# Time mixing in a two-layer decoder trunk: TensorE's rows in program order, weight products cut into units, weights stored in pieces

## The chip, the cores and the metric

The kernel runs on one core of one Trainium2 chip. The metric is device time in microseconds of one execution, the median of several runs. A core has five engines that each work through a queue in order: TensorE (PE, with its weight loads as PEld), VectorE (DVE), ScalarE (ACT), GpSimd (POOL) and SyncE (SP, which here issues the weight DMAs).

## The reference

The trunk has two layers over 256 tokens of width 1024. Layer 0 is RWKV-7 time mixing with memory attention, then a dense SwiGLU; layer 1 is a chunked gMLP with memory attention, then eight experts. What matters here is layer 0's mixing:

```
p = rms_norm(x) @ w_in               # 2816 columns: r, k, v (768 each), lora 256, q 256
r, k, v, wd, ad, gd = split(token_shift_lerp(p))
step:  s = s * w_t - (s @ kk_t) (kk_t * a_t) + v_t k_t ;  y_t = s @ r_t   # 12 heads, 256 steps
y = (group_norm(y) * lnx_w + lnx_b + bonus(r, k) * v) * g
k_m, v_m = split(rms_norm(mem) @ w_kv_mem[i])             # for both layers i
o = softmax(q @ k_m.T / 8) @ v_m                          # 4 heads, 256 memory tokens
x = x + concat(y, o) @ w_out
```

## The kernel before, in words

Every activation is held transposed, 128 features by 256 tokens. A weight product is done in one of two ways. Split: ACT writes a weight piece's rounded part `hi` (L127), DVE the rest `lo` (L128), and TensorE makes three products (hi with high activations, lo with high, hi with low; `lin_cm`, `lin_tm`). Whole: TensorE multiplies the raw float32 weights directly, each product of which the trace shows as two rows. Split pieces go through four buffers of 128x512 per side, so a piece of the next block waits until TensorE has done with the piece four before it. `project(c0, whole)` loads 256 columns of `w_in` (one megabyte) and gives a function that makes its 2 x 128 output rows; `WHOLE` says which blocks are whole: lora, the first two k blocks, all three v blocks. A raw weight lands in one of two or three buffers by a DMA that SP issues in written order.

The recurrence is done in chunks of 64 tokens, 4 chunks of 12 heads (24 pairs of heads, `NM`). After the k blocks, `ND` holds in-chunk products (`AR`, `BK`; 32x32 tiles); DVE transposes them to `NL` (L597) and solves a triangular system in 15 steps of a product and a reduce each (`prod` L605, `TT` L607), transposes the answer twice (`T` L610, `T32t` L611), and TensorE completes it in three passes of 96 small products, `within` (first `T,W`, then `Z,T32t` and `T32t,Z`, the last two each followed by an addition on DVE). The r blocks give `rT`, `AR` and `bt` on DVE and the bonus sums `mm<-bt,bones`; `G` is 48 products of `AR` and `BK` masked on DVE; the v blocks give `vT`, then `VU`; four rounds build `Q` and `VU`; a loop carries the state `S`; `ys` and `group_norm` give y. Only then are the memory tokens normed and turned (`m_tm`), and `mem_kv` and `mem_attn` run.

All engines but SP are ordered by the framework's scheduler, from the program order and tile dependences; SP keeps the written order. TensorE's rows of this stage are therefore not in program order: r blocks stand among the k blocks' work, and the first v block stands while DVE solves the system.

Of the kernel before, what the change touches and what calls it, by code (L numbers as in the profile page):

```python
# [17 lines left out]
D = 1024  # L18
T = 256
# [11 lines left out]

@with_exitstack
def trunk(ctx: ExitStack, tc: tile.TileContext, a: dict, out: bass.AP, dbg=None, full=True):
    nc = tc.nc
    pe, dve, act, pool, sp = nc.tensor, nc.vector, nc.scalar, nc.gpsimd, nc.sync
    dbg = dbg or (lambda name, ap: None)

# [49 lines left out]
    class Stream:  # L87
# [24 lines left out]
        def fetch_cols(self, w, c0, n):  # L112

            if self.early:
                return self.early.pop(0)
            kk = min(KD, 2048 // n)
            return [self.fetch(w[k * 128:(k + kk) * 128, c0:c0 + n].rearrange("(k p) f -> p k f", p=128))
                    for k in range(0, KD, kk)]
# [32 lines left out]
        def rows(self, w, k0, nk):  # L151

            for k in range(k0, k0 + nk, 2):
                n = min(2, k0 + nk - k)
                v = self.fetch(w[k * 128:(k + n) * 128, :].rearrange("(k p) f -> p k f", p=128))
# [194 lines left out]
    def mem_kv(ws_, i, mh):  # L350

        for p in banks_cm(ws_, a["w_kv_mem"][i], 0, 256, mh, 256):
            act.activation(flat(KT[i]), p, AF.Copy)
        yield
        w = ws.cols(a["w_kv_mem"][i], 256, 256)
# [86 lines left out]
    w_in = a["rwkv_w_in"][0]  # L442
# [14 lines left out]
    def project(c0, whole):  # L457

        if c0 == MIX + 256:
            ws.raws.append(rawb)  # L460
        elif c0 == 2 * MIX:
            ws.raws = [raw0, rawb]
        if not whole:
            if not n1:
                split_n1()
            us = list(ws.blocks(w_in, c0, 256))
        else:
            v = ws.fetch_cols(w_in, c0, 256)[0]

        def products():  # L470
            p = lin_bank()
            for j in range(2):
                o = p[:, j * T:j * T + T]
                if not whole:
                    lin_cm(o, us[j], n1)
                for k in range(KD if whole else 0):
                    mm(o, v[:, k, j * 128:j * 128 + 128], n1f[:, k, :], k == 0, k == KD - 1)
            return p
        return products

    WHOLE = {'l': (1,), 'k': (1, 1, 0), 'v': (1, 1, 1), 'r': (0, 0, 0), 'q': (0,)}
    rawb = lambda: rl.tile([128, 2048], F32, name="rawb", tag="rawb")
    projs = (f() for f in ahead(project(c0 + 256 * i, w) for c0, n in ((2304, "l"), (MIX, "k"), (0, "r"), (2 * MIX, "v"), (2560, "q"))
             for i, w in enumerate(WHOLE[n])))
    lora = rb.tile([128, 2, T], F32, name="lora")
    p = next(projs)
# [46 lines left out]
    for i in range(3):  # L533
        p = next(projs)
# [28 lines left out]
    kstack.close()  # L563

# [47 lines left out]

    def within(left, right):
# [15 lines left out]
    rm = rms(m_tm, bv.rearrange("p b t -> p (b t)")[:, None, :D].to_broadcast([128, 2, D]), False)  # L629
    for i in range(3):  # L630
        p = next(projs)
        pb = mm_bank()
        for j in range(2):
            b = 2 * i + j
            rT = f256("rT")
            lerp(rT, p[:, j * T:(j + 1) * T], b)
            dve.tensor_tensor(AR[:, b, :, 1, :], rT.rearrange("p (c j) -> p c j", c=NC), c4(PD, b), op=ALU.mult)
            t = f256("bt")
            dve.scalar_tensor_tensor(t.rearrange("p (c j) -> p c j", c=NC), AR[:, b, :, 1, :], P("rwkv_r_k", b),
                                     BK[b][:, :, 1, :], op0=ALU.mult, op1=ALU.mult)  # L640
            mm(pb[:, j * T:j * T + T], bones, t, True, True)
        act.activation(bv[:, 2 * i:2 * i + 2, :], pair(pb), AF.Copy)

    G = ra.tile([128, 2, NM, 128], F32, name="G", tag="pack")
    for b in range(NB):
        ps = [acc_bank().rearrange("p (c i) -> p c i", c=NC) for _ in range(2)]
        for c in range(NC):
            for s in range(2):
                h = halves[s]
                mm(ps[s][:, c, :], flat(BK[b][h, c, s:s + 2, :]), flat(AR[h, b, c, :, :]), True, True)  # L650
        for s in range(2):
            dve.tensor_tensor(G[:, s, b * NC:(b + 1) * NC, :], ps[s],
                              gmask[:, None, :].to_broadcast([128, NC, 128]), op=ALU.mult)


    vT = rb.tile([128, NB, T + CH], F32, name="vT")
    for i in range(3):
        p = next(projs)
        for j in range(2):
            lerp(vT[:, 2 * i + j, :T], p[:, j * T:(j + 1) * T], 12 + 2 * i + j)  # L660
    qT = rb.tile([128, 2, T], F32, name="qT")
    act.activation(flat(qT), next(projs), AF.Copy)
    for b in range(0, NB, 2):
        act.activation(vT[:, b:b + 2, T:], vT[:, b:b + 2, 0:CH], AF.Copy)
# [9 lines left out]

    for c in range(1, NC):
        p = mm_bank().rearrange("p (b v) -> p b v", v=CH)
        for b in range(NB):
            for h in halves:
                mm(p[h, b, :], AR[h, b, c, 0, :], ident[h, h], True, True)
        act.activation(AR[:, :, c, 0, :], p[:, :NB, :], AF.Copy)  # L680
    VU = ra.tile([128, 2, NM, CH], F32, name="VU", tag="kr")
    slot = lambda s, c: (c + 1) % NC if s else c
    for b in range(NB):
        p = mm_bank().rearrange("p (w d) -> p w d", w=4)
        for w in range(4):
            f = (w + 3) % 4
            mm(p[:, w, :], vT[:, b, f * CH:f * CH + 128], cent, True, True)
        act.activation(VU[0:64, 1, b * NC:(b + 1) * NC, :], p[0:64, :, 64:128], AF.Copy)
        act.activation(VU[64:128, 0, b * NC:(b + 1) * NC, :], p[64:128, :, 0:64], AF.Copy)
# [10 lines left out]
    for p, (m0, m1) in zip(pz, runs):  # L700
        act.activation(Z2[32:64, m0:m1], p[32:64, :m1 - m0], AF.Copy)
        dve.tensor_copy(Z2[96:128, m0:m1], p[96:128, :m1 - m0])
    pz = banks2()
# [7 lines left out]
    dbg("TT", TT.rearrange("p a b -> p (a b)"))  # L711
    sstack.close()
# [17 lines left out]
    for c in range(NC):  # L730
        if c:
# [19 lines left out]
    for c in range(NC):  # L751
        if c + 1 < NC:
            p = state(acc_bank)
            for b, s, h in heads:
                mm(p[h, b, :], BKt[:, s, b * NC + c, :], VU[:, s, b * NC + slot(s, c), :], b == 0, c == 0 and b == NB - 1, True)
            for b, s, h in heads if c else ():
                mm(p[h, b, :], AR[h, b, c, 0, :], S[c - 1][h, b, :], False, b == NB - 1, True)
            dve.tensor_tensor(S[c], p[:, :NB, :], PC[:, :, c, None].to_broadcast([128, NB, CH]), op=ALU.mult)
        if c:
            p = state(acc_bank)  # L760
# [604 lines left out]
```

## Time and profile before

| | |
|---|---|
| median of 3 runs | 1333.71 us (1330.75 to 1334.09) |
| profiled execution | 1332.82 us, its span 1330.7 us, mean granted TensorE clock 0.985 |
| TensorE busy | 1291.1 us (97%) |
| VectorE / ScalarE busy | 1027.7 us (77%) / 898.1 us (67%) |
| layer 0, time mixing and memory attention | from 44 to 218 us of the span, products with `w_out` behind it |
| dense SwiGLU | about 245 to 435 us |
| gMLP layer and routing | about 435 to 525 us |
| experts | about 525 to 1316 us |

A window row gives the busy time of each engine in a stretch, with the number of its instructions, the granted clock and the DMA engines' mean share. TensorE's products are pipelined and their ends are modelled, so its pace is read from starts or counts.

### The profile page before, as it was taken

Reading aid. Unit: us, or ns where it says so; the run is one execution under the profiler, and the core shown is the slowest. Engines: PE = TensorE matmul, PEld = TensorE weight load, DVE = VectorE, ACT = ScalarE, POOL = GpSimd, SP = SyncE. Lnnn points to the kernel's source line nnn. Section 1 sums busy time; section 2 is a strip of 40 time slices with the busy share of each in tenths; the row PEclk is TensorE's granted clock in tenths of the full one; section 3 lists DMA queues with packets and bytes.
Section 4 is the critical chain, followed back from the end, with each engine's and each line's share of the span. In section 5 each row is a group of like instructions: output and inputs, shape, how many; then the busy total and the mean of one; then the engine's idle time right before and its main releaser. Section 6 shows DMA issues by size and latency. Waiting matters only on the chain. (4 is left out here: it accounts for less than half of the span.)

```text
span 1330.7 us, 22558 instructions
## 1 busy us (share of the span) xinstructions
PE 1291.1 (97%) x9048; PEld 1119.2 (84%) x9048; DVE 1027.7 (77%) x1242; ACT 898.1 (67%) x1165; POOL 20.5 (2%) x47
## 2 busy tenths in 40 slices
PE   8979999999999998999999999999999999999995
PEld 6968989999999888888888888888888888888884
DVE  4774366666645765999987999888999988999995
ACT  6621557644544756887787787778787778787874
POOL 2000000000000100000000000000000000000000
PEclk8998999999999998999999999999999999999998
DMA  5422107555557645899999999999999989999960
GB/s 184 134 91 74 58 33 254 190 191 190 196 188 250 228 165 190 293 356 372 342 355 321 357 358 361 347 344 331 341 358 370 357 330 342 345 357 369 355 256 34
DMA packets 170658, 351.47 MB, mean 264 GB/s; under 512 B 5796, under 2 KB 46848, under 8 KB 170544
## 3 DMA queue, kind: packets, MB, share of 16 engines
q1 hardware_dynamic: 169216, 346.05, 73.8%
q0 software_dynamic: 1280, 3.88, 0.9%
q8 instruction: 73, 1.20, 0.4%
q14 instruction: 41, 0.34, 0.1%
q10 hardware_dynamic: 48, 0.01, 0.0%
HBM read 348.87 MB, written 1.05 MB: 263 GB/s over the span
## 5 line engine op out<-in xcount | busy, mean ns | idle before, releaser
L128 DVE TENSOR_TENSOR lo<-raw,hi 128x1024 fp32r<-128x1024 f32 (+1 forms) x636 | 737.0, 1201 | 139.4 <-ACT hi L127 137.6
L127 ACT ACTIVATE hi<-raw 128x1024 fp32r<-128x1024 f32 (+1 forms) x636 | 643.9, 1043 | 180.6 <-PE gu L58 56.9
L58 PE MATMUL gu<-hi,xh 128*128 128x512 f32 (+1 forms) x768 | 289.4, 377 | 0.0
L58 PE MATMUL gu<-hi,xl 128*128 128x512 f32 (+1 forms) x768 | 289.1, 376 | 0.0
L58 PE MATMUL gu<-lo,xh 128*128 128x512 f32 (+1 forms) x768 | 287.9, 377 | 0.0
L58 PEld LDWEIGHTS gu<-hi,xh 128*128 128x128 f32 x768 | 144.5, 188 | 27.9 <-ACT hi L127 0.2
L58 PEld LDWEIGHTS gu<-hi,xl 128*128 128x128 f32 x768 | 144.3, 188 | 28.1
L58 PEld LDWEIGHTS gu<-lo,xh 128*128 128x128 f32 x768 | 144.3, 188 | 27.4 <-DVE lo L128 0.2
L58 PE MATMUL lin<-nh,hi 128*128 128x256 f32 x528 | 149.5, 283 | 0.7 <-DVE rT L446 0.3
L58 PE MATMUL lin<-nh,lo 128*128 128x256 f32 x528 | 148.5, 282 | 1.0 <-DVE lo L128 1.0
L58 PE MATMUL lin<-nl,hi 128*128 128x256 f32 x528 | 149.1, 283 | 0.0
L58 PE MATMUL py<-hi,hh 128*128 128x512 f32 x352 | 140.4, 399 | 0.0
L58 PE MATMUL py<-hi,hl 128*128 128x512 f32 x352 | 139.5, 396 | 0.0
L58 PE MATMUL py<-lo,hh 128*128 128x512 f32 x352 | 111.1, 397 | 0.0
L58 PEld LDWEIGHTS lin<-nh,hi 128*128 128x128 f32 x528 | 99.5, 188 | 2.8 <-issue 0.7
L58 PEld LDWEIGHTS lin<-nh,lo 128*128 128x128 f32 x528 | 99.5, 188 | 2.1 <-DVE lo L128 1.6
L58 PEld LDWEIGHTS lin<-nl,hi 128*128 128x128 f32 x528 | 99.4, 188 | 0.8 <-issue 0.6
L58 PEld LDWEIGHTS py<-lo,hh 128*128 128x128 f32 x352 | 66.1, 188 | 16.3 <-DVE lo L128 0.5
L58 PEld LDWEIGHTS py<-hi,hh 128*128 128x128 f32 x352 | 66.3, 188 | 14.8
L58 PEld LDWEIGHTS py<-hi,hl 128*128 128x128 f32 x352 | 66.3, 188 | 14.8
L1204 ACT ACTIVATE sil<-gu,gw 128x512 f32<-128x512 f32 (+1 forms) x48 | 31.4, 654 | 42.7 <-PE gu L58 41.4
L225 DVE TENSOR_TENSOR hl<-mm,hh 128x512 fp32r<-128x512 f32 (+1 forms) x48 | 31.0, 647 | 25.8 <-ACT hh L224 25.8
(433 smaller groups left out, 1546.7 us busy)
## 6 DMA issues: line engine op xcount, KB each, us to landing
raw<-in_moe_w_gu SPq DMA_DIRECT2D x174, 1024.0 KB, 6.9
raw<-in_moe_w_down SPq DMA_DIRECT2D x87, 1024.0 KB, 7.3
raw<-in_ffn_w_gu SPq DMA_DIRECT2D x22, 1024.0 KB, 7.0
raw<-in_ffn_w_down SPq DMA_DIRECT2D x11, 1024.0 KB, 4.9
raw<-in_w_out SPq DMA_DIRECT2D x7, 1024.0 KB, 8.0
raw<-in_gmlp_w_in SPq DMA_DIRECT2D x7, 1024.0 KB, 5.2
raw<-in_rwkv_w_in SPq DMA_DIRECT2D x5, 1024.0 KB, 5.3
rawa<-in_rwkv_w_in SPq DMA_DIRECT2D x3, 1024.0 KB, 7.2
```

The costliest lines, as they stand in the source:

```text
L58: pe.matmul(o, l, r, start=start, stop=stop, skip_group_check=loose)
L127: act.activation(h, v, AF.Copy)
L128: dve.tensor_tensor(l, v, h.bitcast(F32), op=ALU.subtract)
L225: dve.tensor_tensor(lo, src, hi.bitcast(F32), op=ALU.subtract)
L1204: at(0, lambda: act.activation(sil, ps[0], AF.Silu, scale=rs), f > 0)
```

## The change

Two parts. First, every big weight is stored on the host side in pieces of 128 partitions by 2048 words, in the order in which the kernel loads them (`lay`, `Laid`, `PIECES`), so that a piece is one contiguous run of 8 KB for each partition where it was 8 runs of 1 KB, 4 of 2 KB or 2 of 4 KB. The pieces, their sizes and the order of the DMAs on SP stay.

Second, in the time mixing TensorE is kept in program order from the end of the k blocks to the end of the memory attention (`order`), and the program there is written anew. Blocks of r, v, q, the memory rows, keys and values become units of a `flow`; `some(flow, 1)` makes half a unit (24 products) between two dependent pieces of work. All v blocks become split. `within` moves behind `G`; the state loop, `ys`, `group_norm`, the attention and the units are listed in `steps_`.

```diff
+PIECES = {
+    "rwkv_w_in": steps(2816, 0, 256), "w_kv_mem": steps(512, 0, 256), "ffn_w_gu": steps(DFF) + steps(DFF, DFF),
...
+def lay(w, cols):
+    for c, n in cols or [(0, w.shape[1])]:
+        v = w[:, c:c + n].reshape(-1, 2048 // n, 128, n)
+        out.append(v.transpose(0, 2, 1, 3).reshape(-1, 128, 2048))
...
-            return [self.fetch(w[k * 128:(k + kk) * 128, c0:c0 + n].rearrange("(k p) f -> p k f", p=128))
-                    for k in range(0, KD, kk)]
+            return [self.fetch(v) for v in w.cols(c0, n)]
...
-    WHOLE = {'l': (1,), 'k': (1, 1, 0), 'v': (1, 1, 1), 'r': (0, 0, 0), 'q': (0,)}
...
+    todo = [project(2304, True)] + [project(MIX + 256 * i, i < 2) for i in range(3)] + [project(256 * i, False) for i in range(3)]
+    todo += [project(2 * MIX + 256 * i, False, values_of(i)) for i in range(3)]
+    todo += [project(2560, False, lambda p: act.activation(flat(qT), p, AF.Copy)), mem_rows()]
+    todo += [f(i) for i in range(2) for f in (mem_keys, mem_values)]
+    flow = (p for units in ahead(begin() for begin in todo) for p in units)
...
     kstack.close()
+    order = ExitStack()
+    order.enter_context(tc.manual_schedule(engines={mybir.EngineType.PE}))
...
+        if b == 1:
+            later[0]()
+        if b % 2 == 0:
+            some(flow, 1)
+        bank_ = mm_bank if b % 2 else acc_bank
...
+    (p0, w0), (p1, w1) = within(GM, T32)
+    act.activation(Z[:, w0], p0, AF.Copy)
+    dve.tensor_copy(Z[:, w1], p1)
+    some(flow, 1)
+    for t, lr in ((T32, (T32t, Z)), (T32t, (Z, T32t))):
...
+    steps_ = [lambda: state_of(0), fill, lambda: state_of(1), lambda: add_state(1), fill, lambda: state_of(2), lambda: add_state(2),
+              fill, lambda: ys(0), fill, lambda: add_state(3), lambda: ys(1), lambda: some(gates, 3), norm(0), fill, lambda: ys(2), fill, norm(0),
+              lambda: ys(3), other, other, norm(1), other, other, fill, norm(1)]
+    steps_ += [fill, fill, fill, other, other, other, other]
+    for f in steps_:
+        f()
+    some(flow, 99)
+    order.close()
```

First place: TensorE around the solved system, before. `raw_1182` and `rawb` are the first two v blocks (whole), `T_704` and `T32t` the solution, `AR,BK` the products for `G`.

```order
L58 MATMUL mm<-bt,bones 128x256
L58 MATMUL lin<-n1f,raw_1182 128x256 x5
L58 MATMUL lin<-n1f,rawb 128x256
L58 MATMUL acc<-T_704,W 32x32 x96
L58 MATMUL acc<-Z,T32t 32x32 x96
L58 MATMUL acc<-T32t,Z 32x32 x96
L58 MATMUL acc<-AR,BK 128x128 x48
L58 MATMUL lin<-n1f,rawb 128x256 x15
```

The same place now, from the bonus sums of the second r block on. A row `lin<-nh,hi` begins 24 products of half a unit, of which the rest is left out.

```order
L103 MATMUL mm<-bt,bones 128x256 x2
L103 MATMUL lin<-nh,hi 128x256
...
L103 MATMUL acc<-AR,BK 128x128 x8
...
L103 MATMUL mm<-AR,BK 128x128 x8
L103 MATMUL acc<-T_706,W 32x32 x96
...
L103 MATMUL acc<-Z,T32t 32x32 x96
L103 MATMUL acc<-T32t,Z 32x32 x96
```

The first v block stood ahead of the solution's passes and `G` behind them; now both bonus sums of the second r block, the first v block, half of the second, and all of `G` stand ahead of the passes.

Second place: VectorE at the end of the solution, before (`rT`, `AR`, `bt` are of the last r block, `vT` of the first v block).

```order
L639 SCALAR_TENSOR_TENSOR bt<-AR,pcol,BK 128x256
L607 TENSOR_REDUCE TT<-prod 128x2x14
L605 TENSOR_TENSOR prod<-TT,NL 128x450
L607 TENSOR_REDUCE TT<-prod 128x2x15
L610 STREAM_TRANSPOSE T_704<-TT 128x32x32
L611 STREAM_TRANSPOSE T32t<-TT 128x32x32
L446 SCALAR_TENSOR_TENSOR vT<-lin,pcol,vT 128x255 x2
```

And now (`rT`, `AR`, `bt` here are of the second r block, `raw_881` the first v block):

```order
L748 SCALAR_TENSOR_TENSOR bt<-AR,pcol,BK 128x256
L720 TENSOR_REDUCE TT<-prod 128x2x15
L489 SCALAR_TENSOR_TENSOR rT<-lin,pcol,rT 128x255
L723 STREAM_TRANSPOSE T_706<-TT 128x32x32
L724 STREAM_TRANSPOSE T32t<-TT 128x32x32
L746 TENSOR_TENSOR AR<-rT,pack 128x4x64
L171 TENSOR_TENSOR lo<-raw_881,hi 128x512
L748 SCALAR_TENSOR_TENSOR bt<-AR,pcol,BK 128x256
L171 TENSOR_TENSOR lo<-raw_881,hi 128x512 x3
```

The last r block's work was done before the two transposes; now the second r block's last `bt` and the first v block's `lo` pieces come behind them.

Third place: ScalarE between the last `ys` and the second group norm, now (`yT`, `mg`, `rg`, `ex` belong to y and its norm, `pr` and `warm` to the softmax):

```order
L267 ACTIVATE mg<-yT 128x3x128
L419 ACT_TABLE_LOAD
L419 ACTIVATE pr,st<-acc,st 128x256 x4
L277 ACT_TABLE_LOAD
L277 ACTIVATE rg<-rg 128x12
L419 ACT_TABLE_LOAD
L419 ACTIVATE pr,st<-acc,st 128x256 x4
L170 ACTIVATE hi<-rawb 128x512
L422 ACT_TABLE_LOAD
L422 ACTIVATE warm<-st 128x1
L170 ACTIVATE hi<-rawb 128x512
L637 ACTIVATE ex<-rg 128x384 x2
```

Before, the same norm stood ahead of all softmax work, without a table load of its own:

```order
L127 ACTIVATE hi<-rawb 128x512
L234 ACTIVATE rg<-rg 128x12
L127 ACTIVATE hi<-rawb 128x512
L526 ACTIVATE ex<-rg 128x384 x2
L353 ACTIVATE kv<-lin 128x512
L127 ACTIVATE hi<-rawb 128x512
L224 ACTIVATE mg<-yT 128x3x128 x2
L127 ACTIVATE hi<-raw_2480 128x512
L376 ACT_TABLE_LOAD
L376 ACTIVATE pr,st<-acc,st 128x256
```

Between the root `rg` and `ex`, for which TensorE's last `ident,ex` waits, stood one split; now two table loads, four exponentials, two splits and `warm` stand there, and two more loads and four exponentials just ahead of the root.

## Rows read from the trace of the kernel before

**Rows 1.** The page: busy time, share of the span, instructions.

```profile
PE 1291.1 (97%) x9048; PEld 1119.2 (84%) x9048; DVE 1027.7 (77%) x1242; ACT 898.1 (67%) x1165; POOL 20.5 (2%) x47
```

**Rows 2.** Windows in the experts' stage: engines busy, clock, DMA share.

```profile
600.00:620.00 20.00, 20.00 (x87) 16.10 (x86) 17.66 (x16) 15.09 (x15) 0.00 (x0) 1.00 1.03 376
1290.00:1310.00 20.00, 20.00 (x87) 16.06 (x86) 18.10 (x16) 14.68 (x14) 0.00 (x0) 1.00 0.00 2
```

**Rows 3.** Waits a DMA ended, 560:1280: total us, times, longest.

```profile
ACT hi L127 <- DMA raw<-in_moe_w_gu: 0.3, 1, 0.3
```

**Rows 4.** Waits a DMA ended, 0:240, piece of the third k block.

```profile
ACT hi L127 <- DMA rawa<-in_rwkv_w_in: 2.2, 1, 2.2
```

**Rows 5.** Windows of layer 0, from the transpose NL to attention's end.

```profile
87.69:102.70 15.01, 7.72 (x578) 7.17 (x578) 5.25 (x8) 1.27 (x3) 0.00 (x0) 0.69 0.22 73
93.40:107.00 13.60, 9.75 (x390) 9.42 (x392) 3.52 (x6) 1.57 (x2) 1.46 (x2) 0.50 0.02 5
102.70:134.50 31.80, 30.53 (x207) 27.35 (x207) 14.69 (x25) 7.33 (x14) 1.46 (x2) 0.93 0.29 94
134.50:169.30 34.80, 34.09 (x942) 31.85 (x941) 12.71 (x24) 18.20 (x39) 0.00 (x0) 1.00 0.13 39
169.30:217.70 48.40, 46.57 (x467) 41.05 (x468) 30.77 (x73) 32.25 (x75) 0.00 (x0) 1.00 0.25 83
```

**Rows 6.** Timeline of VectorE: start, us, what; the solution's transposes.

```profile
64.98 2.08 DVE L597 STREAM_TRANSPOSE NL<-ND 128x1024 f32<-128x1024 f32 x1
...
85.59 1.95 DVE L610 STREAM_TRANSPOSE T<-TT 128x1024 f32<-128x1024 f32 x1
87.44 1.92 DVE L611 STREAM_TRANSPOSE T32t<-TT 128x1024 f32<-128x1024 f32 x1
```

**Rows 7.** VectorE by line, 67:85.6: count, busy us, mean ns, idle.

```profile
L605 DVE TENSOR_TENSOR prod<-TT,NL 128x2 f32<-128x2 f32 (+14 forms) x15 | 6.6, 442 | 0.2
L607 DVE TENSOR_REDUCE TT<-prod 128x2 f32<-128x2 f32 (+14 forms) x15 | 4.9, 323 | 0.2
L639 DVE SCALAR_TENSOR_TENSOR bt<-AR,pcol,BK 128x256 f32<-128x256 f32 x6 | 2.9, 481 | 0.0
L637 DVE TENSOR_TENSOR AR<-rT,pack 128x256 f32<-128x256 f32 x6 | 2.5, 416 | 0.0
L446 DVE SCALAR_TENSOR_TENSOR rT<-lin,pcol,rT 128x255 f32<-128x255 f32 x5 | 2.4, 479 | 0.1
L128 DVE TENSOR_TENSOR lo<-rawa,hi 128x512 fp32r<-128x512 f32 x3 | 2.1, 695 | 0.0
```

**Rows 8.** Timeline of TensorE: last wait in the passes, G.

```profile
101.10 1.60 PE L58 MATMUL acc<-T32t,Z 32*32 32x32 f32 x101 [1.53 <-issue]
...
109.66 1.53 PE L58 MATMUL acc<-AR,BK 64*128 64x128 f32 x16 [0.20 <-DVE G L652]
```

**Rows 9.** Waits of TensorE, 63:240: total us, times, longest.

```profile
PE acc L58 <- issue: 6.1, 3, 2.5
```

**Rows 10.** Timeline of TensorE: the third v block, whole.

```profile
120.79 7.07 PE L58 MATMUL lin<-n1f,raw 128*128 128x256 f32 x32
```

**Rows 11.** Windows of tile lin alone: split products.

```profile
213.50:229.30 15.80, 15.80 (x132) 15.80 (x132) 0.68 (x1) 0.58 (x1) 1.00 1.07 374
```

**Rows 12.** Timeline of ScalarE: norm's copies, table load, exponential, split.

```profile
193.95 0.94 ACT L224 ACTIVATE mg<-yT 128x384 fp32r<-128x384 f32 x2 [0.75 <-DVE yT L809]
...
197.44 1.28 ACT L376 ACT_TABLE_LOAD   x1
...
204.04 0.48 ACT L376 ACTIVATE pr<-acc,st 128x256 f32<-128x256 f32 x1 [0.27 <-DVE st L374]
...
205.86 0.64 ACT L127 ACTIVATE hi<-rawb 128x512 fp32r<-128x512 f32 x1
```

**Rows 13.** Timeline of TensorE: scores of the softmax.

```profile
194.36 1.13 PE L58 MATMUL acc<-kv,qT 64*128 64x256 f32 x4
```

**Rows 14.** Timeline of TensorE: sums of squares.

```profile
187.28 1.48 PE L58 MATMUL mm<-bones,W 128*128 128x2 f32 x12
```

More of the change, by code (lines that the diff above doesn't have):

```diff
@@ L481, in trunk, with project, begin, products @@
-    WHOLE = {'l': (1,), 'k': (1, 1, 0), 'v': (1, 1, 1), 'r': (0, 0, 0), 'q': (0,)}
-    rawb = lambda: rl.tile([128, 2048], F32, name="rawb", tag="rawb")
-    projs = (f() for f in ahead(project(c0 + 256 * i, w) for c0, n in ((2304, "l"), (MIX, "k"), (0, "r"), (2 * MIX, "v"), (2560, "q"))
-             for i, w in enumerate(WHOLE[n])))
+    def project(c0, whole, done=None):
+        def begin():
+            if c0 == MIX + 256:
+                ws.raws.append(rawb)
+            elif c0 == 2 * MIX:
+                ws.raws = [raw0, rawb]
+            if not whole:
+                if not n1:
+                    split_n1()
+                us = list(ws.blocks(w_in, c0, 256))
+            else:
+                v = ws.fetch_cols(w_in, c0, 256)[0]
+            def products():
+                p = lin_bank()
+                for j in range(2):
+                    o = p[:, j * T:j * T + T]
+                    if not whole:
+                        lin_cm(o, us[j], n1)
+                    for k in range(KD if whole else 0):
+                        mm(o, v[:, k, j * 128:j * 128 + 128], n1f[:, k, :], k == 0, k == KD - 1)
+                    if j == 0:
+                        yield None
+                if done:
+                    done(p)
+                yield p
+            return products()
+        return begin
@@ new lines, in mem_keys, with begin, products, mem_values @@
+    def mem_keys(i):
+        def begin():
+            us = list(ws.blocks(laid("w_kv_mem", i), 0, 256))
+            def products():
+                p = lin_bank()
+                for j in range(2):
+                    lin_cm(p[:, j * T:j * T + T], us[j], mh)
+                    if j == 0:
+                        yield None
+                act.activation(flat(KT[i]), p, AF.Copy)
+                yield p
+            return products()
+        return begin
+    def mem_values(i):
+        def begin():
+            w = ws.cols(laid("w_kv_mem", i), 256, 256)
+            def products():
+                p = pair(lin_bank())
+                for m in range(2):
+                    lin_tm(p[:, m, :], w, mh, m * 128)
+                    if m == 0:
+                        yield None
+                act.activation(VM[i], p, AF.Copy)
+                yield p
+            return products()
+        return begin
@@ L627, in trunk @@
             dve.tensor_tensor(t[:, w], p, t[:, w], op=ALU.add)
[L629 to L664, printed above, removed]
+    some(flow, 1)
     BKt = ra.tile([128, 2, NM, CH], F32, name="BKt", tag="ba")
@@ L702, in trunk @@
         dve.tensor_copy(Z2[96:128, m0:m1], p[96:128, :m1 - m0])
+    for c in range(1, NC):
+        p = mm_bank().rearrange("p (b v) -> p b v", v=CH)
+        for b in range(NB):
+            for h in halves:
+                mm(p[h, b, :], AR[h, b, c, 0, :], ident[h, h], True, True)
+        act.activation(AR[:, :, c, 0, :], p[:, :NB, :], AF.Copy)
     pz = banks2()
@@ L711, in trunk @@
     dbg("TT", TT.rearrange("p a b -> p (a b)"))
+    some(flow, 1)
+    VU = ra.tile([128, 2, NM, CH], F32, name="VU", tag="kr")
+    slot = lambda s, c: (c + 1) % NC if s else c
+    for b in range(NB):
+        p = mm_bank().rearrange("p (w d) -> p w d", w=4)
+        for w in range(4):
+            f = (w + 3) % 4
+            mm(p[:, w, :], vT[:, b, f * CH:f * CH + 128], cent, True, True)
+        act.activation(VU[0:64, 1, b * NC:(b + 1) * NC, :], p[0:64, :, 64:128], AF.Copy)
+        act.activation(VU[64:128, 0, b * NC:(b + 1) * NC, :], p[64:128, :, 0:64], AF.Copy)
     sstack.close()
@@ L849, in mixed @@
             yield c0 // 128
-    early = [ws.fetch_cols(a["w_out"][0], c0, 256) for c0 in (0, 256)]
+    early = [ws.fetch_cols(laid("w_out", 0), c0, 256) for c0 in (0, 256)]
     astack.close()
@@ L856, in trunk @@
     ws.raws = raws1
-    early += [ws.fetch_cols(a["w_out"][0], c0, 256) for c0 in (512, 768)]
+    early += [ws.fetch_cols(laid("w_out", 0), c0, 256) for c0 in (512, 768)]
     ws.early = early
@@ L884, in trunk @@
         for part in range(2):
-            for j, p in enumerate(banks_cm(ws, a["ffn_w_gu"][0], part * DFF + 128 * i, 128 * n, n2)):
+            for j, p in enumerate(banks_cm(ws, laid("ffn_w_gu", 0), part * DFF + 128 * i, 128 * n, n2)):
                 if part == 0:
```

232 lines of the change are left out of this document (135 added, 97 removed).

## The prediction

> **What bounds the kernel now.** I read the page's first part, then windows. TensorE is busy for 97% of the span [rows 1], so what can be won lies in its few waits, and the question is where each half of the change meets them. In the experts' stage two windows of 20 us hold the same 87 products, once at a DMA share of 1.03 and once at 0.00, and TensorE is never idle in either [rows 2]; in 560:1280 one wait of 0.3 us ended with a transfer [rows 3]. In layer 0, from 0 to 240 us, the one wait for a transfer inside a dependent chain is 2.2 us [rows 4]. TensorE's idle time in layer 0 is elsewhere: in the solution's passes it is busy for 7.72 of 15.01 us, and 0.7 to 1.8 us are idle in each later window [rows 5]. 6.1 us of it, in three waits inside the passes, are named "issue" [rows 9]: no other engine ended them. With them the granted clock falls from its 2.4 GHz level to the 1.2 GHz one, and stays there to 107 us [rows 5].
>
> **The layout.** It changes no instruction's size and no order of DMAs. The experts can gain the 0.3 us of [rows 3] and layer 0 at most the 2.2 us of [rows 4], part of which other products cover. I take 0, with -2 to 0 as its bounds. The Trainium skill ("DMA: Bandwidth & Descriptors", section "Latency and other measured facts") says that a row pitch of a large power of two in HBM can halve the transfer rate, and that tiles laid out contiguously avoid it; by that rule the transfers get faster, and the trace says only that TensorE does not wait for them [rows 2]. It is rival D.
>
> **Time mixing, up to the passes.** In program order no r product may run among the k blocks, and VectorE, which there feeds the solution, loses the `lo` pieces of an r block: NL starts about 1.5 us earlier than 64.98 [rows 6] (two pieces of 0.695 [rows 7] lie just ahead of it on the path), at 63.4.
>
> VectorE then solves the system. Before, its work between the transposes was 6.6 + 4.9 + 2.9 + 2.5 + 2.4 + 2.1 = 21.4 us [rows 7], done between 67.06 and 85.59, in 18.5 us [rows 6]: instructions overlap, by a factor of 0.865. Now it is the same recursion, 11.5; eight `lo` of the second and third r block, 8 x 0.695 = 5.6; four `rT`, 4 x 0.479 = 1.9; three `AR`, 1.25; three `bt`, 1.45: 21.7, by the factor 18.8 us. New is that `rT` waits in this queue for r products that before had been made long ago, and the recursion queues behind it: 0 to 4.2 us (the second r block's products can't end before those of the first, 2 x 5.75 us behind the k stage; see below), 1.5 taken, since most of the recursion comes first. The transposes take 2.08 at its head and 3.8 at its end: `T32t` is done at 63.4 + 2.1 + 18.8 + 1.5 + 3.8 = 89.6, against 89.36 before [rows 6]. The chain gains nothing.
>
> TensorE has only three r blocks to fill these 26 us. A split block is 48 products; 132 took 15.80 us [rows 11], so 0.12 each and 5.75 a block, 17.3 for three. Of the 26.2 us to 89.6 some 8 are idle, the last of them just before `T32t`: the bonus sums of the second r block wait for a `bt`, and the first v block's units for `lo` pieces, which stand behind both transposes on VectorE. Before, that v block stood here. So from 89.6 on TensorE does in order: `bt` and its sums (1.4 + 0.5), the first v block (5.75), half of the second (2.9), `G`, 6 x 1.53 = 9.2 [rows 8], and the third block's bonus sums (0.5): 20.2. After an idle stretch the clock may be low: before, the low level lasted from the last such wait, ended at 101.10 [rows 8], to 107.0, 5.9 us, half of which is lost; so 0 to 3, 1.5 taken. `G` and the units end at 111.3.
>
> **The passes.** Now they stand behind `G`, with half a unit (2.9) between the first and the second. Before they took 15.01, of which 6.1 "issue" [rows 5, 9]. The low bound is their products without those waits and at the full clock, 5.6, and the unit: 8.5. The high bound is 15.0 as before. The waits came where some 576 rows of 32x32 [rows 5] follow each other at some 16 ns each (1.60 us for 101 [rows 8]); no engine's result is awaited, so the new place of the passes doesn't take them away, and 24 longer products only relieve one of three. I take 13.9, near the upper row: 125.2. Another half unit (2.9) follows: 128.1.
>
> **To the rounds.** Before, by 134.5 `G`, all v blocks and q were done [rows 5]. Now the second half of the third v block (2.9) and q (5.75) are still missing at 128.1: 136.8. The split v blocks are cheaper on TensorE: 5.75 against 7.07 whole [rows 10], and that is in these figures. But they bring 12 `hi` on ScalarE, 0.64 each [rows 12], and 12 `lo` on VectorE, 0.695 each [rows 7], 7.7 and 8.3 us, in a queue whose other entries TensorE waits for in order: 0 to 3, 1.3 taken. At this point the kernel is 136.8 + 1.3 - 134.5 = 3.6 us late.
>
> **Behind the rounds.** The memory rows, keys and values stand between the state's dependent products. TensorE is idle there for 0.71 + 1.83 us [rows 5]; I take 1.9 of these 2.5 as filled (0.5 to 2.5). A new wait comes at the second norm. TensorE's last `ident,ex` needs ScalarE's `ex`, ahead of which now stand, behind the last `ys`: `mg` 0.47, four table loads of 1.28, eight exponentials of some 0.45 (four from 204.04 to 205.86), a root 0.2, two `hi` at 0.6, `warm` 0.2, `ex` 0.5 [rows 12], in all 11.3. TensorE has beside it, before `ident,ex`: scores 2 x 1.13 [rows 13], sums of squares 0.74 (half of [rows 14]), half a key block 2.9: 5.9, and up to 9.3 if the last `ys` and what is queued with it is still to be done when ScalarE starts. The wait is 2.0 to 5.4; I take 4.1, as ScalarE's start itself hangs on the first norm's last additions. It covers nothing, since TensorE's order is fixed and the products behind it are its own. The clock behind it: 0 to 1.7 lost, 0.9 taken. The Trainium skill ("ScalarE: Activation LUTs", section "What ACT_TABLE_LOAD costs") gives each switch of the table 2.66 us, 1.28 of load and 1.38 of drain; the row shows the 1.28, with the next activation at 198.74, 0.02 behind its end in the trace. By the page the wait would be some 2.8 us longer; rival C.
>
> **The sum.** 3.6 - 1.9 + 4.1 + 0.9 + 0 (layout) = +6.7 us. From `w_out` on TensorE is the bound as before and the delay stays. The profiled execution of before took 1332.82 us, so 1339.5; the median of the runs is 0.9 above it: forecast 1340.4, say 1340. All low ends together: 1.5 + 1.5 + 5.4 + 1.3 + 0.6 + 2.1 + 0.9 + 2 = 15.3 below, 1325. All high ends: 2.7 + 1.5 + 1.1 + 1.7 + 1.4 + 1.3 + 0.8 = 10.5 above, 1351.
>
> **Rivals.**
> A, no change. The passes lose their "issue" waits because other work stands before and in them: 8.5 instead of 13.9, and the sum is +1.3, 1335. For it: the half unit lies where the first of them was. Against: these waits show no releaser at all, and two passes still follow each other directly.
> B, faster. The units do what gaps are filled with: no issue waits (-5.4), no low clock behind an idle stretch (-1.5 and -0.9), VectorE's queue doesn't wait for r products (-1.5), and the wait at the second norm is at its low end, 2.0 (-2.1): 6.7 - 11.4 = -4.7, so 1329, or down to 1325 with the rest. It decides once the r blocks' products run no later than the recursion asks for them and the passes aren't limited by their own issue. For it: 7.3 us of idle time and 13.6 us at the low clock stand in 87 to 107 [rows 5]. Against: the first v block, which filled the gap before, can't come there now.
> C, the table switches cost more than the loads show: 2.8 more, 1343.
> D, the experts wait for transfers in a way that shows as a slower pace and not as a wait: contiguous pieces then shorten them. Were it 1% of the 791 us of that stage, 8 us, the sum is -1, at 1333; at 2%, 1325. Against it: 87 products with the DMA share at 1.03 and at 0.00 [rows 2]; even one product in 87 fewer without DMA would be 1%.
> E, the forecast's mechanism at its high end: the recursion's waits for r products and ScalarE's queue both at their upper bound, 1345 to 1351.
>
> **How the numbers follow.** A measurement of this kernel tells some 0.3%, 4 us, from no change: 1329.7 to 1337.7. The chances: the forecast 0.40, A 0.24, B 0.20, C 0.06, D 0.04, E 0.06. B and half of D are faster, 0.22; A and the lower edge of the forecast's own spread (0.04) no change, with the other half of D 0.30; the rest slower, 0.48. The slower case has its own range, 1338 to 1350. Since cases of both signs hold much of the chance, the range that is to hold the time 8 times in 10 goes from 1326, which is B near its lower end, to 1349, where one in ten is left on each side.
>
> **What would show it.** In the profile after: `T32t` ending at 88 to 92; TensorE idle for several us just ahead of the first v block, with a low clock at the start of `G`; waits named "issue" in the passes again, and the passes with their unit 12 to 15 us long; a wait of 2 to 5 us at the last `ident,ex`, ended by ScalarE; the experts' windows with 87 products each as before. I am wrong if the passes take under 10 us, if TensorE has no gap ahead of `G`, or if the experts' stage gets shorter.

## The result: slower, 1352.07 us, and the profile after

The changed kernel takes 1352.07 us (median of 4 runs, 1350.97 to 1353.53) against 1333.47 before: the ratio is 1.0144, with a 95% interval of 1.0127 to 1.0162. The forecast was slower too, but at 1340 with a range of 1326 to 1349, and the time lies above that range.

The profiled execution has a span of 1350.7 us, 20.0 more than before. All of it arises in layer 0: the last product with `w_out` starts at 264.63 us where it was 243.37 (+21.3), the first gate product of the experts at 549.01 where it was 527.15, the last at 1304.27 where it was 1282.44. From the first gate product to the last it is 755.3 us in both. About 2 us come back in the output behind the last product (12.1 us where it was 14.0). The windows of the changed kernel, by its own stages (us, then busy time and instructions of TensorE, its weight loads, VectorE, ScalarE, GpSimd, then the granted clock, the DMA share and GB/s):

```profile
44.00:66.28 22.28, 16.53 (x280) 15.03 (x279) 14.88 (x39) 15.12 (x38) 1.47 (x3) 0.73 0.28 100
66.28:91.22 24.94, 19.59 (x149) 18.56 (x148) 24.42 (x52) 10.15 (x19) 0.00 (x0) 0.97 0.23 85
91.22:112.73 21.51, 19.96 (x174) 18.32 (x174) 16.41 (x30) 6.60 (x12) 0.00 (x0) 0.84 0.27 99
112.73:129.29 16.56, 9.61 (x602) 9.01 (x600) 6.80 (x13) 3.00 (x6) 0.00 (x0) 0.79 0.19 67
133.85:189.30 55.45, 54.54 (x1122) 51.25 (x1122) 23.89 (x44) 29.76 (x62) 0.00 (x0) 0.97 0.11 40
189.30:221.60 32.30, 26.83 (x259) 23.15 (x257) 18.32 (x47) 21.51 (x48) 0.00 (x0) 0.89 0.19 66
221.60:264.80 43.20, 41.91 (x312) 38.43 (x311) 24.78 (x41) 25.98 (x53) 0.00 (x0) 0.96 0.56 217
621.80:641.80 20.00, 20.00 (x87) 16.10 (x86) 17.66 (x16) 15.11 (x15) 0.00 (x0) 1.00 1.01 397
1311.80:1331.80 20.00, 20.00 (x87) 16.05 (x87) 18.10 (x16) 14.73 (x14) 0.00 (x0) 1.00 0.01 2
```

The last two rows are those of [rows 2], moved by 21.8 us: 87 products with and without transfers, as before. The first row is the surprise: in the k stage (the k blocks' work, up to the transpose `NL`) TensorE is idle for 5.75 us and runs at a mean clock of 0.73, where before it was busy for 19.82 of 20 us at the full clock. Over the whole stretch from 44 us to the end of `w_out`, TensorE's idle time went from 13.8 to 27.3 us and its busy time from 185.7 to 193.5, though three split v blocks take about 4 us less than three whole ones: the mean granted clock there fell from 0.97 to 0.90. The rows behind these comparisons, the k stage before, the whole stretch before, and the whole stretch now:

```profile
44.00:64.00 20.00, 19.82 (x330) 18.88 (x332) 16.73 (x43) 16.33 (x40) 1.48 (x3) 1.00 0.32 107
44.00:243.50 199.50, 185.74 (x2864) 170.18 (x2863) 121.74 (x251) 100.90 (x224) 2.94 (x5) 0.97 0.32 105
44.00:264.80 220.80, 193.53 (x2911) 178.17 (x2910) 130.62 (x264) 114.32 (x240) 2.93 (x5) 0.90 0.26 97
```

The changed kernel's waits from 44 to 265 us (total us, times, longest), which answer to [rows 9]:

```profile
PE acc L103 <- issue: 7.0, 3, 3.5
PE mm L103 <- DVE bt L748: 6.6, 3, 5.0
PE mm L640 <- ACT ex L637: 4.9, 3, 1.8
PE acc L103 <- DVE BK L671: 1.7, 1, 1.7
PE mm L103 <- DVE bv L887: 1.5, 1, 1.5
PE acc L103 <- ACT pr L419: 1.4, 1, 1.4
```

Before, no other kind than the issue waits of [rows 9] (6.1 us in three) came to more than 1.2 us in all:

```profile
PE mm L58 <- DVE bv L776: 1.2, 1, 1.2
```

Windows of the changed kernel around and behind three of its waits (columns as above):

```profile
52.00:68.00 16.00, 10.25 (x225) 9.03 (x225) 10.26 (x25) 8.23 (x22) 1.47 (x3) 0.57 0.04 13
92.00:96.00 4.00, 3.50 (x14) 3.32 (x15) 3.93 (x9) 1.07 (x2) 0.00 (x0) 0.50 0.17 33
212.00:220.00 8.00, 6.80 (x28) 5.76 (x28) 4.53 (x16) 7.91 (x20) 0.00 (x0) 0.63 0.00 0
```

A granted clock of 0.50 is the 1.2 GHz level. In the second row's stretch the split products start 0.21 us apart, where the full clock has 0.12 ([rows 11]). So work behind a wait takes longer too; what that is worth to the end of the stage is asked below.

The two chains of the forecast, as VectorE's and TensorE's timelines of the changed kernel show them (start, us, what; in brackets the idle time before and what ended it):

```profile
66.28 2.02 DVE L710 STREAM_TRANSPOSE NL<-ND 128x1024 f32<-128x1024 f32 x1 [1.34 <-ACT ND L708]
...
89.36 1.86 DVE L724 STREAM_TRANSPOSE T32t<-TT 128x1024 f32<-128x1024 f32 x1
```

```profile
92.50 1.22 PE L103 MATMUL mm<-bt,bones 128*128 128x256 f32 x2 [4.98 <-DVE bt L748]
...
112.73 1.85 PE L103 MATMUL acc<-T,W 32*32 32x32 f32 x192
...
120.78 0.76 PE L103 MATMUL acc<-Z,T32t 32*32 32x32 f32 x64 [1.94 <-issue]
...
125.60 1.93 PE L103 MATMUL acc<-T32t,Z 32*32 32x32 f32 x128 [3.49 <-issue]
...
129.06 0.31 PE L103 MATMUL acc<-T32t,Z 32*32 32x32 f32 x2 [1.53 <-issue]
```

The solution ends at 91.2 (89.36 in [rows 6]); TensorE waits 4.98 us just ahead of the first v block, as the forecast said; the passes take 16.6 us and keep their three issue waits.

ScalarE's timeline at the second norm:

```profile
209.69 1.28 ACT L419 ACT_TABLE_LOAD   x1 [1.13 <-DVE st L417]
210.99 0.47 ACT L419 ACTIVATE pr<-acc,st 128x256 f32<-128x256 f32 x1
...
212.94 1.28 ACT L277 ACT_TABLE_LOAD   x1
214.23 0.21 ACT L277 ACTIVATE rg<-rg 128x12 f32<-128x12 f32 x1
214.46 1.28 ACT L419 ACT_TABLE_LOAD   x1
...
218.23 1.28 ACT L422 ACT_TABLE_LOAD   x1
219.52 0.20 ACT L422 ACTIVATE warm<-st 128x1 f32<-128x1 f32 x1
...
220.15 0.92 ACT L637 ACTIVATE ex<-rg 128x384 f32<-128x384 f32 x2
```

Four loads of 1.28 us, and the next activation 0.01 to 0.02 us behind the end of each: rival C's longer switch isn't here.

### The profile page after: what moved, and what is told of

It reads as the page before. It is cut to its first block, busy times and chain, and to the rows that moved or that the text cites. A ratio compares the mean times of both kernels' runs of the same rounds, so it can differ in the third digit from the quotient of the medians.

```text
span 1350.7 us, 22699 instructions
## 1 busy us (share of the span) xinstructions
PE 1300.3 (96%) x9096; PEld 1129.1 (84%) x9096; DVE 1036.8 (77%) x1254; ACT 910.7 (67%) x1179; POOL 20.5 (2%) x47
## 3 DMA queue, kind: packets, MB, share of 16 engines
q0 software_dynamic: 1280, 3.88, 0.9%
## 5 line engine op out<-in xcount | busy, mean ns | idle before, releaser
L103 PE MATMUL lin<-nh,hi 128*128 128x256 f32 x576 | 168.0, 292 | 0.1
L103 PE MATMUL lin<-nh,lo 128*128 128x256 f32 x576 | 165.0, 287 | 0.7 <-DVE lo L171 0.7
L103 PE MATMUL lin<-nl,hi 128*128 128x256 f32 x576 | 164.6, 286 | 0.0
L103 PEld LDWEIGHTS lin<-nh,hi 128*128 128x128 f32 x576 | 112.5, 195 | 2.3 <-issue 1.0
L103 PEld LDWEIGHTS lin<-nh,lo 128*128 128x128 f32 x576 | 112.6, 195 | 1.4 <-DVE lo L171 0.9
L103 PEld LDWEIGHTS lin<-nl,hi 128*128 128x128 f32 x576 | 112.3, 195 | 0.7 <-issue 0.6
```

The costliest lines, as they stand in the source:

```text
L103: pe.matmul(o, l, r, start=start, stop=stop, skip_group_check=loose)
```

## The experiments

The theory from this trace: the fixed order on TensorE makes it wait where other work used to stand, each wait lowers the clock behind it, and the layout does nothing. The rivals: the layout costs or gains; the rewritten program (split v, `G` ahead of the passes, softmax inside the norm) costs in any order; the waits cost their idle time alone.

Times are medians with intervals; the ends of stages come from one profiled execution of each kernel. These executions differ by some us before the changed stretch begins: the later of the two rows `acc<-bones,sqk` of the second k block starts at 51.45 us in the kernel before, at 52.34 in the changed one, and anywhere from 48.80 to 52.83 in the others, where the granted clock from 27 to 35 us was 1.00 (48.80) and 0.57 (52.83). Counted from there to the last product with `w_out`, the kernel before takes 191.9 us (191.8 with the layout alone), the changed one 212.3. Below, such counts are called "counted from the k products".

**The layout alone.** The program of before, with the weights stored and loaded as in the changed kernel.

```diff
-            return [self.fetch(w[k * 128:(k + kk) * 128, c0:c0 + n].rearrange("(k p) f -> p k f", p=128))
-                    for k in range(0, KD, kk)]
+            return [self.fetch(v) for v in w.cols(c0, n)]
```

> The program of before with the weights stored in pieces, nothing else. Theory (TensorE is the bound of the experts and never waits for a transfer there): the time of before, 1333.5 within 2 us, and the experts' stage as long as before (755 us between the first and the last gate product). Rival (contiguous pieces shorten the experts): under 1330. Second rival (the layout itself is what costs): up to 1352, as the changed kernel.

1331.24 against 1331.76 us: ratio 1.000 (0.9986 to 1.0014), 755.2 us from the first gate product to the last. The transfers did change, as the DMA rows of the pages show, the kernel before first:

```profile
DMA packets 170658, 351.47 MB, mean 264 GB/s; under 512 B 5796, under 2 KB 46848, under 8 KB 170544
DMA packets 50082, 351.47 MB, mean 264 GB/s; under 512 B 5796, under 2 KB 5888, under 8 KB 8240
```

The median time from issue to landing fell too, from 6.9 to 6.6 us for the experts' gate pieces and from 8.0 to 6.2 for those of `w_out`. Whether that is for the reason that the prediction named, rows that lie a large power of two apart, isn't shown: the rows of these weights lay 2 to 22 KB apart. It gained nothing, since TensorE did not wait for transfers. Neither of the two rivals holds, and D is out.

**No fixed order.** The changed kernel with the scheduler placing TensorE's rows ("freely placed" below).

```diff
-    order.enter_context(tc.manual_schedule(engines={mybir.EngineType.PE}))
...
-    order.close()
```

> The changed kernel without the fixed order on TensorE: the same program text, the scheduler places TensorE's rows again. Theory (the fixed order costs: r and v products can't run in the k stage and beside the solution, the gaps idle and lower the clock): idle time of 44 to 92 us falls from 12 us to 3, and the time to 1336 to 1342. Rival (the rewritten program costs, with its split v blocks, G ahead of the passes and the softmax inside the second norm): 1348 to 1353.

1326.59 us, ratio 0.9951 (0.9935 to 0.9968): faster than expected, and faster than before. The rewritten program is not what costs. Its windows for the k stage and for everything to the end of `w_out`:

```profile
44.00:65.48 21.48, 21.30 (x344) 20.26 (x344) 18.11 (x46) 17.36 (x43) 1.47 (x3) 1.00 0.28 100
...
44.00:238.90 194.90, 185.32 (x2906) 171.75 (x2906) 127.74 (x264) 111.66 (x239) 2.93 (x5) 0.96 0.30 109
```

The k stage is full again, and the last product with `w_out` starts at 238.71, 25.9 us ahead of the changed kernel (25.5 counted from the k products). ScalarE still has the four table loads and eight exponentials ahead of the second norm's `ex` here, the loads at 194.03, 197.28, 198.80 and 203.02, and TensorE has no wait for `ex`: that chain costs nothing where other products can stand beside it.

**The order in parts.** First, fixed only from `G` to the end of the attention (the comments in the two cuts are put in here to say where a line stands):

```diff
-    order.enter_context(tc.manual_schedule(engines={mybir.EngineType.PE}))   # behind the k blocks
+    order.enter_context(tc.manual_schedule(engines={mybir.EngineType.PE}))   # ahead of G
```

> The changed kernel, its fixed order on TensorE begun only ahead of G, so that the r blocks may run among the k blocks. Theory (the k stage's gap and its low clock are worth 4 to 6 us by themselves): 1346 to 1348. Rival (the gap only moves: r products done earlier leave TensorE idle for longer beside the solution, since the first v block still can't come there): 1350 to 1353.

1343.36 us, ratio 1.0089 (1.0068 to 1.0110), `w_out`'s last product at 256.11: the order in the k stage and beside the solution is worth 8.5 us, more than expected. The rival's shift is there too, since a wait of 5.5 us stands in `G` now. The solution itself ends later here, at 94.9 for 91.2, as VectorE has 11 split pieces and six `bt` beside the recursion, where the changed kernel has eight and three. So what the order cost here was not a later solution; it points to TensorE's own idle time and low clock, since work that it didn't do in the k stage it had to do later.

Then the rest of it in two halves: from `G` to the rounds, and from the state loop to the end of the attention.

```diff
+    order.close()                                  # ahead of steps_: the first half
+    order.enter_context(tc.manual_schedule(engines={mybir.EngineType.PE}))   # ahead of steps_: the second
```

> The changed kernel with the fixed order on TensorE from G to the end of the rounds only; before and behind the scheduler places the rows. By the runs so far the freely placed program takes 1326.6 and the one fixed from G to the end of the attention 1343.4. Theory (each fixed stretch costs its own waits and the low clock behind them): the wait of 5.5 us in G and the low clock behind it stay, the second norm's waits go: 1334 to 1337. Rival (the cost lies behind the rounds): 1327 to 1329. Rival (it lies in G and the passes): 1341 to 1344.

> The changed kernel with the fixed order only for the state loop, the norms and the attention. Theory (waits at the gates, the softmax and the second norm, 5.5 us, and a low clock behind them): 1333 to 1337, and with the fixed order from G to the rounds it adds up to the 17 us between 1326.6 and 1343.4. Rival (TensorE would wait there anyway): 1326 to 1329.

1333.58 (ratio 1.0001, 0.9983 to 1.0019), just under its range, and 1340.74 us (1.0063, 1.0043 to 1.0084), above its own. `w_out`'s last product starts at 244.04 and 249.65, so 5.3 and 10.9 us later than without an order. The three parts, 8.5 + 5.3 + 10.9 = 24.7, make up all but 1.2 us of the 25.9; counted from the k products they are 8.3, 5.1 and 11.8 of 25.5. By the ratios they are 0.0055, 0.0050 and 0.0112 of 0.0193, which adds up within the intervals. The largest waits that the two halves bring, total us, times, longest; first half, from 44 us on (without an order `G` had 1.4 in three):

```profile
PE mm L103 <- DVE G L767: 5.6, 1, 5.6
```

second half, from 150 us on:

```profile
PE mm L640 <- ACT ex L637: 2.1, 1, 2.1
PE mm L103 <- DVE bv L884: 1.5, 1, 1.5
PE acc L103 <- ACT pr L419: 1.3, 1, 1.3
PE sum L103 <- ACT pr L436: 0.7, 1, 0.7
PE mm L103 <- DVE yT L917: 0.5, 1, 0.5
PE lin L103 <- ACT oh L267: 0.5, 1, 0.5
```

With one of 0.3 us for `W`, which was there without an order too, these come to 6.9; 10.9 - 6.6 = 4.3 us of this half are not waits. Most of them can be the clock: its mean from 150 us to the end of `w_out` is 0.95 over 99.8 us here and 0.98 over 88.9 without an order, some 3 us at half speed (an estimate).

**The clock by itself.** Products of ones, whose results nothing uses, fill the 5 us gap ahead of the second block's bonus sums.

```diff
+        if i == 2:
+            p = sum_bank()
+            for _ in range(22):
+                mm(p[:, :128], ones, ones, True, True)
         for f in later:
             f()
```

> The changed kernel with 22 products of ones by ones (128x128, result unused) in TensorE's queue between the third r block and the bonus sums that wait 5 us for VectorE. They compute nothing that is used. Theory (the gap costs twice, as idle time and as a low clock behind it from 92 to 99 us): the clock stays at its full level and the next half unit takes 2.9 us where it took 5.5: 1348.5 to 1350. Rival (the gap costs its idle time alone): 1352, or some us more if the products overfill it.

The time, 1350.70 us (ratio 1.0127, 1.0103 to 1.0150), can't be told from the changed kernel's 1.0144. The trace can: in this window, which read 0.50 in the changed kernel, the clock is full,

```profile
92.00:96.00 4.00, 3.33 (x25) 2.88 (x25) 3.93 (x9) 1.22 (x3) 0.00 (x0) 1.00 0.03 4
```

the passes begin at 110.80 instead of 112.73, though the solution ended 0.7 us later, and the last product with `w_out` starts at 262.17 instead of 264.63. 22 useless products made the stage 2.5 us shorter. Other traces agree: counted from the k products, the first norm's last turn (`ident,ex`) starts after 151.4 and 150.9 us in the two kernels that have the same rows up to there and no useless products (the changed one and the one with the norm first, below), and after 148.8 and 148.5 in the two that have them. The same in three gaps:

```diff
+        if c0:                      # behind the second norm's sums
+            for _ in range(6):
+                mm(p[:, 128:256], ones, ones, True, True)
...
+            if c0 and b == 0:       # ahead of the last norm's turn
+                for _ in range(10):
+                    mm(p[:, 0, :], ones, ones, True, True)
```

> The changed kernel with products of ones that compute nothing used, in three of the gaps of TensorE's fixed order: 22 ahead of the bonus sums that wait 5.0 us, 6 ahead of the scores that wait 1.4 us, 10 ahead of the last norm's turn that waits 1.8 us. Theory (behind each gap the low clock costs as much again; with 22 products alone w_out ended 2.4 us earlier): the half unit behind the scores takes 3.1 us where it took 4.8, and w_out ends 5 to 6 us earlier than in the changed kernel, at about 259; 1346 to 1348. Rival (low clock there has another cause than the gaps): the half unit stays at 4.8, 1350 to 1352.

1349.84 us (ratio 1.0128, 1.0103 to 1.0153), above the 1346 to 1348 of the theory. The half unit behind the scores takes 3.1 us where it took 4.8, at the full clock:

```profile
208.00:214.00 6.00, 6.00 (x42) 5.11 (x41) 3.18 (x13) 5.93 (x15) 0.00 (x0) 1.00 0.00 0
```

but what it wins is given to the next wait, since `ex` comes when ScalarE's chain is done: that wait is 2.2 us even behind ten products more, and `w_out`'s last product starts at 262.27, not at about 259. There the clock costs little beyond the chain; the theory's "as much again" holds for the first gap and not for this one.

**The second norm ahead of the softmax**, in the fixed order.

```diff
-              lambda: ys(3), other, other, norm(1), other, other, fill, norm(1)]
+              lambda: ys(3), norm(1), fill, norm(1), other, other, other, other]
```

> The changed kernel, in its fixed order, with the second group norm taken ahead of all softmax scores. Theory (the table loads and exponentials ahead of the norm's copies hold up TensorE's turn by 1.8 us, the scores' banks by 1.4, and the clock falls behind): the wait for ex is under 0.5 us and 3 to 6 us go: 1346 to 1349. Rival (the norm now waits for VectorE and ScalarE in the same way, and the softmax's waits only come later): 1351 to 1354.

1356.48 us, ratio 1.0183 (1.0158 to 1.0207): no gain, as the rival had it, and above the rival's range (1351 to 1354) as well. The trace is of the fastest of its four executions (1351.69); in it layer 0 takes 212.3 us counted from the k products, as in the changed kernel. The norm's wait for `ex` is gone and the waits move to the scores' banks:

```profile
PE acc L103 <- ACT pr L419: 5.3, 1, 5.3
...
PE sum L103 <- ACT W L906: 1.4, 1, 1.4
```

The chain of softmax and norm on ScalarE has to be covered by TensorE's work, and in a written order it is covered only by what was written beside it.

**Units between the passes' small products**, in the freely placed version; TensorE's order is fixed in the passes alone.

```diff
         for m in range(NM):
+            if m == NM // 2:
+                some(flow, 1)
...
     for t, lr in ((T32, (T32t, Z)), (T32t, (Z, T32t))):
         for p, w in within(*lr):
             dve.tensor_tensor(t[:, w], p, t[:, w], op=ALU.add)
-    some(flow, 1)
+        some(flow, 1)
```

> The freely placed version with TensorE's order fixed in the three passes alone and a half unit of 24 long products behind every 48 small ones, five instead of one between the first and the last. Theory (the waits named issue come from the supply of instructions, some 128 rows every 3.5 to 4.8 us, and long products give it time): no such wait is left in the passes, the clock stays at its full level, 6.9 us of waits and some 3 us of low clock go: 1317 to 1321. Rival (the waits belong to the passes themselves): the waits stay, 1326 to 1328, or later if the rounds now lack the units.

1322.70 us, ratio 0.9934 (0.9910 to 0.9958): the best of all, though not told apart from 0.9951 by its interval, and short of the expected 1317 to 1321. The trace shows what was gained. TensorE's passes, with 24 long products between two rows:

```profile
100.90 1.05 PE L103 MATMUL acc<-T,W 32*32 32x32 f32 x96
...
104.94 1.02 PE L103 MATMUL acc<-Z,T32t 32*32 32x32 f32 x96
...
108.95 1.05 PE L103 MATMUL acc<-Z,T32t 32*32 32x32 f32 x96
...
112.99 1.02 PE L103 MATMUL acc<-T32t,Z 32*32 32x32 f32 x96
```

No row has a wait; the 6.9 us of issue waits that the freely placed version has are gone, and the clock stays full. The passes' stretch is longer for the units in it, and those are missing from the gaps later, where up to 2.5 us of waits for norm and softmax come in between 190 and 222 us, at a mean clock of 0.84. Counted from the k products, 3.0 us are left of the 10 that were hoped for.

What ends an issue wait can be read from the traces as well. The page of the changed kernel has a DMA queue for instructions:

```profile
q8 instruction: 73, 1.20, 0.4%
```

73 packets of 16 KiB fit TensorE's 9096 products and as many weight loads: some 250 instructions a packet, or 125 rows with their loads (an estimate from these counts), and 128 rows stand between one issue wait and the next in the changed kernel. In the records of this queue, every one of the 36 issue waits in and just behind the passes, in the 13 traces that have any, ends 1.2 to 1.5 us behind the end of such a packet; in the changed kernel the packets end at 119.29, 124.32 and 127.69, the waits at 120.78, 125.60 and 129.06. So these waits are for TensorE's own instructions, as the expectation supposed.

**Whole v blocks**, without an order, and with the spread passes, and these with the norm ahead of the softmax.

```diff
-    todo += [project(2 * MIX + 256 * i, False, values_of(i)) for i in range(3)]
+    todo += [project(2 * MIX + 256 * i, True, values_of(i)) for i in range(3)]
```

> The freely placed version of the changed kernel with the three v blocks whole as before. Theory (split v saves 1.3 us of TensorE's time a block, and its pieces fit beside other work when the scheduler places them): 4 us slower, 1330 to 1332. Rival (the 12 pieces on VectorE hold up the solution, which ends at 93.0 there and ended at 89.4 before): faster, 1323 to 1326.

> The freely placed version with half units between every 48 small products of the passes and whole v blocks. Theory (both are good for themselves: no issue waits, 12 pieces fewer on VectorE, so the solution ends earlier): 1317 to 1321. Rival (the gains overlap, since the earlier solution only meets the same total of work on TensorE, with v 4 us longer): 1322 to 1325.

> As the former, with the second group norm ahead of the softmax in the program. Theory (TensorE waits for the norm and the softmax by some 2 us there): 1 to 2 us less than the former. Rival (freely placed, the scheduler hides it either way): the same within 1 us.

1324.89 (ratio 0.9949, 0.9936 to 0.9962), 1326.48 (0.9949, 0.9931 to 0.9966) and 1327.05 us (0.9956, 0.9939 to 0.9973). The first time lies in the rival's range, but against 0.9951 with split blocks it is no gain: whole or split v makes no difference that can be measured. 4 us more of products stand against a solution that ended at 88.4 instead of 95.0 (the 93.0 of the expectation is where its last transpose starts). 3.2 us of that are no gain of the blocks, since NL starts at 62.3 for 65.5 and the k products ahead of it are already 3.1 us earlier in this execution. The gains of spreading and of whole blocks don't add up, as the rival had it, and the time is above the rival's range too. Two short issue waits are left in that version, of 0.5 us each. The norm ahead of the softmax changes nothing measurable here either.

## Why the prediction was wrong

The direction and the cause (program order makes TensorE wait for VectorE and ScalarE) were right; the size was about a third of what came, 6.7 us against 18.6. Step by step, against the terms of its sum:

- **Layout 0**: right (1.000).
- **Solution done at 89.6**: 91.2. The step that failed is "NL starts about 1.5 us earlier": it starts 1.3 us later. 0.9 of that stand already in the k products ahead of the order, which differ so much between executions (51.42 in the run with the norm first, whose rows are the same up to there); from these to NL it is 13.9 us now and 13.5 before. I took pieces off VectorE and looked no further, but they were not what NL waited for. Now VectorE is idle for 1.34 us ahead of it and waits for ScalarE's `ND`, and that for TensorE's last `acc<-AR,BK`. And with no r product among the k blocks TensorE itself waits there (for `BK`, `ex`, `sqk`) and falls to the low clock: 0.57 from 52 to 68 us. The wait of the recursion for r products, 1.5 taken, gave part of it back.
- **From there to the passes**: 21.5 us against 21.7 (20.2 and 1.5 for the clock). The sum is right, but by luck: the half unit behind the 5 us wait took 5.5 us for 2.9, so the clock cost 2.6 where I took 1.5, and `G` took 6.9 where I had 9.2. The rows of 1.53 that I took for `G` had waits for VectorE's masks between them before [rows 8].
- **Passes 13.9**: 16.6. The unit relieved none of the issue waits: they were 7.0 us where they had been 6.1. The upper bound, 15.0, was too low, since it had no place for the unit. And the next half unit ran at the low clock behind them, 4.6 us against 2.9. The run with units between all halves shows what would have removed them.
- **To the rounds, 2.3 us late before the queues are counted** (136.8 against 134.5): by the same reckoning 133.85 + 2.9 + 5.75 = 142.5, so 8.0. The difference, 5.7, is the terms above.
- **Behind the rounds**: 1.3 - 1.9 + 4.1 + 0.9 = 4.4 forecast, 21.3 - 8.0 = 13.3 measured. This is the largest miss. The new wait at the last `ident,ex` came and is 1.8 us, under the 2.0 to 5.4 that I had for it; with the one ahead of it, 1.4 at the scores' banks, it makes 3.2. What I left out are the waits of the same kind around them, at `bv`, `yT`, `pr` and `oh` (1.5, 0.5, 0.7, 0.5), which the freely placed version hasn't got: other products stand there. TensorE's idle time from the rounds to the end of `w_out` is 7.7 us, against 2.5 before, where the sum had it up by 2.2. And the clock, 0.9 taken, is 0.97, 0.89 and 0.96 in the three stretches from 133.85 us to the end of `w_out`, where it was 1.00 from the rounds on ([rows 5]). At half speed for that share it is some 7 us at most, an estimate. Here the clock is the term that was most too small.

So two sizes failed: I charged an order that is fixed over some 175 us at the three places that I had looked at, where many more dependent steps without a written filler became waits, in the k stage and behind the rounds; and I put the low clock at 2.4 us in all. Of the rivals, A and B both had the issue waits gone, and they stayed. The rewritten program is 0.5% faster as soon as the order isn't fixed, but not for B's reasons: its issue waits are 6.9 us there.

What stays open: which part of the rewritten program gains these 0.5% (not the layout, and by the times not split v), whether spreading the passes gains anything beyond the freely placed version, and how the clock's loss divides between the places behind the first gap, since the products that filled two more gaps moved the end of `w_out` by nothing. Fixing TensorE's order can change the order on the other engines too; no run separates the two.

## What to carry to other kernels

Fixing an engine's order takes away every filler that isn't written down: list all steps of the stretch whose operand comes from another engine, and find for each the independent work that stands just ahead of it, before fixing anything. Price a gap on TensorE twice, by its idle time and by the work that runs at the low clock behind it, unless a chain on another engine ends later anyway. A run of hundreds of small products is best spread among long ones: here the issue waits went from 6.9 us to none, though the time didn't move beyond its interval. And before one trace of each kernel is compared, a place ahead of the change is looked for from which to count: here the single executions differed by up to 4 us there.

## What the runs showed of the hardware

- Useless work can bring the end of a stage forward: 22 products in a gap of 5 us kept the granted clock at 1.00 where it had been 0.50 from 92 to 96 us, and the stage ended 2.5 us earlier. The kernel's time moved by less than its interval (1.0127 against 1.0144).
- A long run of 32x32 products outruns the supply of TensorE's instructions. In the changed kernel three waits named "issue" stand in 576 rows, ending at 120.8, 125.6 and 129.1 us, the last two 128 rows apart, and each 1.3 to 1.5 us behind the end of a 16 KiB packet of the instruction queue. With 24 products of 0.13 us behind every 96 rows there was none; with whole v blocks between them two of 0.5 us were left.
- A table load on ScalarE takes 1.28 us, and the next activation starts 0.01 to 0.02 us behind it.
- A third of the packets for the same bytes (170658 to 50082) changed the time by nothing measurable (1.000, 0.9986 to 1.0014), in a kernel whose TensorE is busy for 97% of the time.
